# The first block's attention on one core: last queries' scores in the output's bank, and four due times moved

## The chip, the cores and the metric

The kernel runs on one core of one Trainium2 chip. The metric is the device time of one execution in microseconds. TensorE does the matrix products, VectorE (DVE), ScalarE (ACT) and GpSimd (POOL) the rest, SyncE (SP) issues most loads. Each engine works through its own queue in order and waits at semaphores for the others.

## The reference, cut to what matters

Two transformer blocks run one behind the other on 512 tokens of width 1024. The change touches only the attention of the first block: 16 heads of width 64, 16 meta tokens ahead of the 512, a forget gate that adds a difference of running sums to the scores, and an output gate.

```python
def _fox_attend(q_blk, c_q, pos_q, k, v, c_k, pos_k):
    s = jnp.einsum('bhqd,bhkd->bhqk', q_blk, k).astype(jnp.float32) * (FOX_HEAD_DIM ** -0.5)
    s = s + (c_q[..., :, None] - c_k[..., None, :])
    s = jnp.where(pos_k[None, :] <= pos_q[:, None], s, -jnp.inf)
    p = jax.nn.softmax(s, axis=-1)
    return jnp.einsum('bhqk,bhkd->bhqd', p, v.astype(jnp.float32))
```

Queries and keys are normalized per head (mean square, root, gain) before that. Behind it the output is multiplied by `sigmoid(gate)`, goes through `fox_w_out`, and a feed-forward part follows. The second block (gated linear attention and a mixture of 64 experts) isn't touched.

## The kernel before

The method `fox` does the attention. The heads go in eight pairs `t`. For each pair TensorE projects the query (512 columns, one bank), the key and the value (528 columns, two banks each) and the gate (512, one bank), eight pieces of three or six products each; `project` yields after each piece. After each piece a `Weave` advances by one step and runs what is due in that step: `at(delay, fn)` puts a function so many steps ahead. A pair takes 32 steps. The numbers `F_V` to `F_0` in one line of the file, and `K_0` and `Q_1` for the first pairs, are those delays; nothing else sets the order. Each function issues its instructions on all the engines at once, so that its place in the step list is its place in every queue.

- `got_q`, `got_k`: evacuate the projection on VectorE (L392), square on ScalarE (L394) and POOL (L396, L397: a high part and the rest of the square). `root` (due `Q_U` or `K_U` steps later) sums the squares per head on TensorE (`sums`, L323) into a bank `tp`, and starts the root (L222 to L226 on ScalarE, L224 on VectorE). `scaled` (due `Q_R` or `K_R` later) ends the root (L229, L230) and scales the query or key (L406).
- `got_v`: evacuates the value (L416) and transposes it after `F_V` steps (L422, L425, bank `tp`).
- `got_g`: evacuates the gate (L462) and works out its sigmoid in three parts, due `F_G`, `F_G + 2` and `F_G + 6` steps later: L467 and L468 on ScalarE, L472 on ScalarE with L473 and L474 on POOL, L477 on ScalarE.
- `attend(t)`: eight units u = 2i + s (query block i of 128, head s of the pair), one every two steps. `scores` makes the scores in a bank `py` (L502 mask, L504, L506), their maximum on VectorE (L510, L512), the exponential with its sum on ScalarE (L515); `scaled` divides by the sum (L520 to L523, two steps later). The last block's rows are 528 wide, more than a bank, and go in two halves: the second into a bank `tp`. `flip`, eight steps behind `scores`, transposes the probabilities into `tp` (L535) and copies them out (L537 on ScalarE or L539 on VectorE, chosen by `F_E`). `values(i)` multiplies them with the values into the bank `plog` (L547), `F_O` and two steps behind the flips of the block's first head; `gated` multiplies the output by the gate (L553).
- Weights: each chunk's high part is made on ScalarE (L170), its low part on VectorE (L180).

PSUM has eight banks: `mm` three, `py` two, `tp` two, `plog` one. A function that takes a bank waits until what was in it has been read.

Of the kernel before, what the change touches and what calls it, by code (L numbers as in the profile page):

```python
# [20 lines left out]
F32 = mybir.dt.float32  # L21
# [9 lines left out]
P = 128  # L31
D = 1024
KT = D // P
T = 512
# [35 lines left out]

A_W, A_Q, A_K, A_R = 1, 1, 2, 5

F_E = 1, 1, 1, 1, 1, 0, 0, 0


F_V, Q_U, Q_R, Q_H, Q_L, K_U, K_R, K_H, K_L, F_S, F_F, F_O, F_G, F_N, F_0 = 6, 3, 2, 12, 1, 2, 2, 6, 2, 12, 8, 4, 12, 2, 5

K_0, Q_1 = (7, 2, 10, 2), (5, 2, 12, 1)


class Weave:
# [5 lines left out]
    def at(self, delay, fn, *args):  # L87
        self.todo.setdefault(self.step + delay, []).append((fn, args))
# [11 lines left out]
class Net:  # L100
# [147 lines left out]
    def fox(self):  # L248
# [9 lines left out]
        pp = self.pp  # L258

        def mm():  # L260
            return pp.tile([P, T], F32, name="mm", bufs=3)
# [86 lines left out]
        def f_bank():  # L348
            return pp.tile([P, T], F32, name="py", bufs=2)
# [34 lines left out]
        at = w.at  # L384
# [28 lines left out]
        def got_v(t, pv):  # L413
            v1 = wk.tile([P, TM], F32, name="v1", bufs=1)
            for p, o, n in pv:
                nc.vector.tensor_mul(v1[:, o:o + n], p, r1[:, o:o + n])  # L416

            def flip():
                vt = vts[t % 2]
                tp = pp.tile([P, T], F32, name="tp", bufs=2)  # L420
                for j in range(NB):
                    nc.tensor.transpose(tp[:, j * P:(j + 1) * P], v1[:, j * P:(j + 1) * P], self.ident)  # L422
                nc.scalar.activation(vt[:, 0:NB].rearrange("p j d -> p (j d)"), tp, AF.Copy)
                tp = pp.tile([P, T], F32, name="tp", bufs=2)
                nc.tensor.transpose(tp[:NM, :P], v1[:, T:TM], self.ident)  # L425
                nc.vector.tensor_copy(vt[:NM, NB], tp[:NM, :P])

            at(F_V, flip)

        def got_q(t, pq):  # L430

# [54 lines left out]
        def attend(t):  # L486
            vt = vts[t % 2]
            pts, po = [], []

            def scores(i, s):  # L490
                kw = NM + P * (i + 1)
                qi = slice(i * P, (i + 1) * P)
                ps = pp.tile([P, T], F32, name="py", bufs=2)
                if kw > T:
                    n = kw // 2
                    pieces = [(ps, 0, n), (pp.tile([P, T], F32, name="tp", bufs=2), n, n)]
                else:
                    pieces = [(ps, 0, kw)]
                for p, o, n in pieces:
                    m0 = max(o, kw - P)  # L500
                    if m0 < o + n:
                        nc.tensor.matmul(p[:, m0 - o:n], self.identb, self.maskb, start=True, stop=False,  # L502
                                         skip_group_check=True)
                    nc.tensor.matmul(p[:, :n], qs[:, s, qi], kd[:, s, o:o + n], start=(m0 >= o + n), stop=False,  # L504
                                     skip_group_check=True)
                    nc.tensor.matmul(p[:, :n], q2[:, s, qi], k2[:, s, o:o + n], start=False, stop=True,  # L506
                                     skip_group_check=True)
                mx = wk.tile([P, 6], F32, name="mx", bufs=4)
                for e, (p, o, n) in enumerate(pieces):
                    nc.vector.tensor_reduce(mx[:, e:e + 1], p[:, :n], axis=AX.X, op=OP.max, negate=True)  # L510
                if len(pieces) > 1:
                    nc.vector.tensor_tensor(mx[:, 0:1], mx[:, 0:1], mx[:, 1:2], op=OP.min)  # L512
                for e, (p, o, n) in enumerate(pieces):
                    c = pt_off[i] + o
                    nc.scalar.activation(pb[s][:, c:c + n], p[:, :n], AF.Exp, bias=mx[:, 0:1],  # L515
                                         accum_out=mx[:, 2 + e:3 + e])

                def scaled():
                    if len(pieces) > 1:
                        nc.vector.tensor_add(mx[:, 2:3], mx[:, 2:3], mx[:, 3:4])  # L520
                    nc.vector.reciprocal(mx[:, 4:5], mx[:, 2:3])
                    pbi = pb[s][:, pt_off[i]:pt_off[i] + kw]
                    nc.vector.tensor_scalar(pbi, pbi, mx[:, 4:5], None, op0=OP.mult)  # L523

                at(F_N, scaled)

            def flip(i, s):
                if i == 0:
                    pts.append(wk.tile([P, PW], F32, name=f"pt{s}", bufs=1))
                for j0 in range(0, i + 2, 4):  # L530
                    n = min(4, i + 2 - j0) * P
                    c = pt_off[i] + j0 * P
                    tp = pp.tile([P, T], F32, name="tp", bufs=2)
                    for o in range(0, n, P):
                        nc.tensor.transpose(tp[:, o:o + P], pb[s][:, c + o:c + o + P], self.ident)  # L535
                    if F_E[2 * i + s]:
                        nc.scalar.activation(pts[s][:, c:c + n], tp[:, :n], AF.Copy)  # L537
                    else:
                        nc.vector.tensor_copy(pts[s][:, c:c + n], tp[:, :n])  # L539

            def values(i):
                if i == 0:
                    po.append(pp.tile([P, T], F32, name="plog", bufs=1))
                for j in range(i + 2):
                    c = pt_off[i] + j * P
                    for s in range(2):
                        nc.tensor.matmul(po[0][s * HD:(s + 1) * HD, i * P:(i + 1) * P],  # L547
                                         vt[:, j, s * HD:(s + 1) * HD], pts[s][:, c:c + P],
                                         start=(j == 0), stop=(j == i + 1), skip_group_check=True)

            def gated():
                sg = sgs[t]
                nc.vector.tensor_mul(sg, po[0], sg)  # L553
                nc.scalar.activation(ogh[:, t], sg, AF.Copy)

            def gated_lo():
                sg = sgs.pop(t)
                nc.vector.tensor_sub(ogl[:, t], sg, ogh[:, t].bitcast(F32))

            s0 = F_S + (0 if t else F_0)  # L560
            for u in range(2 * NB):
                at(s0 + 2 * u, scores, u // 2, u % 2)
                at(s0 + F_F + 2 * u, flip, u // 2, u % 2)
            for i in range(NB):
                at(s0 + F_F + F_O + 4 * i + 2, values, i)
            at(s0 + F_F + F_O + 4 * NB, gated)
            at(s0 + F_F + F_O + 4 * NB + 2, gated_lo)

        kinds = ((got_q, False), (got_k, True), (got_v, True), (got_g, False))
        forget_1()  # L570
        got_q(0, q0)
# [15 lines left out]
        for n in range(self.EARLY):  # L587
            p = mm() if n < 3 else f_bank()
# [16 lines left out]
        for m in range(KT):  # L605
            if m < self.EARLY:
                p = early[m]
            else:
                p = mm()
# [1041 lines left out]
```

## Time and profile before

| | us |
|---|---|
| median of three runs | 1423.62 |
| lowest, highest | 1423.37, 1426.2 |
| the profiled execution, as timed | 1424.26 |
| its span in the trace | 1422.6 |
| TensorE busy, of the span | 1353.3 (95%) |
| VectorE busy | 742.4 (52%) |
| ScalarE busy | 535.8 (38%) |
| POOL busy | 144.1 (10%) |

The page gives the busy time of each engine and in how much of each fortieth of the span it was busy. TensorE is at nine tenths or more from the third fortieth on; ScalarE and VectorE are at six to eight tenths in the first nine and fall off after that. The first nine fortieths are the attention of the first block. The DMA engines are nearly full only in the last third, the experts.

### The profile page before, as it was taken

To read this page: it belongs to the slowest core of one execution; us is meant where nothing else is said; L and a number is where in the kernel's file an instruction comes from. 1 tells how busy PE (TensorE), PEld (TensorE's weight loads), DVE (VectorE), ACT (ScalarE), POOL (GpSimd) and SP (SyncE) were. 2 spreads that over 40 slices of the span, in tenths; PEclk is the share of its full clock that TensorE was granted. 3 is DMA by queue.
4 is the path that set the end of the run, shared out by engine and by line. 5 is a ranking of instruction groups with operands and counts; after the bars stand their busy time and mean duration, and the time that the engine had idled before them with its cause. 6 is when DMAs were issued, how large, how long until landed. Compare 5 with 4: busy or idle time off the path is not lost.

```text
span 1422.6 us, 20730 instructions
## 1 busy us (share of the span) xinstructions
PE 1353.3 (95%) x8506; PEld 1027.8 (72%) x8506; DVE 742.4 (52%) x1321; ACT 535.8 (38%) x988; POOL 144.1 (10%) x127
## 2 busy tenths in 40 slices
PE   7899999999999999999999999999989999999994
PEld 6788888888788888888887888876556555555542
DVE  7887778774654433444456576542233332333343
ACT  6766666664523212333443444522111111111113
POOL 2212222211200000000322122000000000000001
PEclk9999999999999999999999999999989999999998
DMA  4111111113332322232221223698998999999995
GB/s 168 65 40 60 60 61 60 60 60 119 119 108 89 119 89 89 89 108 99 90 89 63 85 89 118 265 390 351 399 413 347 420 420 421 420 420 421 419 420 213
DMA packets 41346, 282.26 MB, mean 198 GB/s; under 512 B 4736, under 2 KB 4992, under 8 KB 7840
## 3 DMA queue, kind: packets, MB, share of 16 engines
q1 hardware_dynamic: 40464, 280.05, 49.8%
q8 instruction: 68, 1.11, 0.3%
q10 hardware_dynamic: 784, 0.85, 0.2%
q14 instruction: 30, 0.25, 0.0%
HBM read 278.72 MB, written 2.10 MB: 197 GB/s over the span
## 4 chain that ended last, share of the span: by engine, by line
PE 75%; DVE 9%; DMA 8%; ACT 4%; issue 1%; POOL 1%; SPq 0%; ACTq 0%; DVEq 0%; POOLq 0%
PE mm L207 20%; PE mm L336 8%; PE py L207 8%; PE tp L207 8%; PE tp L1269 7%; DMA wring<-in_w_dram 6%; PE mm L1357 6%; PE py L1301 3%; PE mm L792 2%; PE mm L1287 2%; PE mm L1288 2%; PE tp L1280 1%; DMA wraw<-in_w_dram 1%; DVE pb L523 1%; PE plog L547 1%
## 5 line engine op out<-in xcount | busy, mean ns | idle before, releaser
L180 DVE TENSOR_TENSOR whl<-wraw,whl 128x1024 fp32r<-128x1024 f32 x138 | 181.6, 1316 | 102.4 <-ACT whl L170 102.2
L336 PE MATMUL mm<-xh,whl 128*128 128x264 f32 (+1 forms) x736 | 183.4, 333 | 3.8 <-DVE q L392 2.8
L170 ACT ACTIVATE whl<-wraw 128x1024 fp32r<-128x1024 f32 x138 | 144.5, 1050 | 109.6 <-PE mm L207 45.8
L207 PE MATMUL mm<-xh,whl 128*128 128x512 f32 x544 | 175.9, 397 | 0.0
L336 PEld LDWEIGHTS mm<-xh,whl 128*128 128x128 f32 x736 | 120.8, 191 | 19.0 <-issue 3.4
L1269 PEld LDWEIGHTS tp<-h,xt 128*128 128x128 f32 x1024 | 115.9, 192 | 6.1 <-PE mm L1357 2.5
L207 PEld LDWEIGHTS mm<-xh,whl 128*128 128x128 f32 x544 | 102.2, 188 | 23.2 <-issue 2.3
L1269 PE MATMUL tp<-h,xt 128*128 128x128 f32 x1024 | 118.5, 276 | 0.2 <-DVE h L1260 0.2
L207 PE MATMUL mm<-xl,whl 128*128 128x512 f32 x272 | 106.0, 390 | 0.0
L336 PE MATMUL mm<-xl,whl 128*128 128x264 f32 (+1 forms) x368 | 100.1, 325 | 0.0
L1307 DVE SCALAR_TENSOR_TENSOR h<-py,sv,h 128x512 fp32r<-128x512 f32 (+1 forms) x33 | 24.2, 735 | 137.9 <-ACT h L1304 137.9
L1357 PE MATMUL mm<-wring,h 128*32 128x512 f32 x664 | 76.7, 595 | 2.3 <-ACT h L1272 2.0
L1289 DVE TENSOR_TENSOR acc<-acc,mm 128x512 f32<-128x512 f32 (+1 forms) x120 | 73.7, 672 | 7.8 <-PE mm L1288 7.6
L1272 ACT ACTIVATE h<-tp,vecs 128x128 f32<-128x128 f32 x128 | 36.6, 369 | 104.8 <-PE tp L1269 104.8
L1369 ACT ACTIVATE tmp<-mm,sv 128x256 f32<-128x256 f32 x16 | 7.6, 474 | 179.5 <-PE mm L1357 164.4
L207 PE MATMUL mm<-ogh,whl 128*128 128x512 f32 x224 | 73.7, 396 | 0.0
L1287 PE MATMUL mm<-h,ss 128*128 128x512 f32 (+1 forms) x128 | 62.6, 490 | 9.4 <-DVE acc L1289 6.4
L635 POOL TENSOR_TENSOR ss<-ss,sq 128x512 f32<-128x512 f32 x21 | 29.2, 1405 | 371.1 <-ACT sq L631 349.1
L207 PE MATMUL py<-xh,whl 128*128 128x512 f32 x208 | 65.8, 391 | 0.0
L207 PE MATMUL tp<-xh,whl 128*128 128x512 f32 x208 | 65.2, 389 | 0.0
L336 PEld LDWEIGHTS mm<-xl,whl 128*128 128x128 f32 x368 | 62.3, 191 | 3.1
L207 PEld LDWEIGHTS mm<-xl,whl 128*128 128x128 f32 x272 | 51.1, 188 | 11.5 <-issue 1.4
(429 smaller groups left out, 2472.2 us busy)
## 6 DMA issues: line engine op xcount, KB each, us to landing
wring<-in_w_dram SPq DMA_DIRECT2D x124, 1024.0 KB, 19.8
wraw<-in_wd_dram SPq DMA_DIRECT2D x69, 1024.0 KB, 4.8
whl<-in_w_dram SPq DMA_DIRECT2D x27, 1024.0 KB, 16.3
v<-in_w_dram SPq DMA_DIRECT2D x20, 1024.0 KB, 17.6
wraw<-in_w_dram SPq DMA_DIRECT2D x18, 1024.0 KB, 19.8
h<-in_xT_dram SPq DMA_DIRECT2D x8, 256.0 KB, 5.8
acc<-in_w_dram SPq DMA_DIRECT2D x2, 1024.0 KB
out_dram<-wring SPq DMA_DIRECT2D x4, 512.0 KB, 4.5
```

What stands on the lines that cost most here:

```text
L170: self.nc.scalar.activation(hl[:, 0], raw, AF.Copy)
L180: self.nc.vector.tensor_sub(hl[:, 1], raw, hl[:, 0].bitcast(F32))
L207: self.nc.tensor.matmul(out, w, x[:, first + k], start=(at + k == 0 and e == 0), stop=(at + k == of - 1 and e == 2))
L336: nc.tensor.matmul(p[:rows, :m], w[:, wi, k], xx[:, k, o:o + m], start=(n == 0), stop=(n == 3 * KT - 1))
L635: nc.gpsimd.tensor_add(ss, ss, sq)
L792: nc.tensor.matmul(pv[b], x[:, k, bs], w2[:, wi, k % 2], start=(k == 0 and e == 0), stop=(k == KT - 1 and e == 2))
L1269: nc.tensor.matmul(p[:, k], self.xt[:, b, (k0 + k) * P:(k0 + k + 1) * P], oh[:, 1, b], start=(b + k == 0), stop=(b == NB - 1), skip_group_ ...
L1272: nc.scalar.activation(xs[:, k0 + k], p[:, k], AF.Copy, scale=self.vec(V_FN2, k0 + k))
L1287: nc.tensor.matmul(pc, gt[:, b * P:(b + 1) * P], yh[:, hs], start=True, stop=False)
L1289: nc.vector.tensor_add(acc[b][:, hs], acc[b][:, hs] if q else self.xt[:, b, hs], pc)
L1301: nc.tensor.matmul(py[js, o:o + c], hT[:, e, js], w, start=(e == 0), stop=(e == 1), skip_group_check=True)
L1357: nc.tensor.matmul(ps[32 * j:32 * j + 32], xs[:, k, 32 * j:32 * j + 32], self.ring[q, k][:, j * T:(j + 1) * T], start=(k == 0), stop=(k == ...
```

## The change

Six numbers and three places in the code:

- `V_0 = 8`: the first pair's values are transposed eight steps behind their projection, not six.
- `Q_U` 3 to 4, `K_U` 2 to 3: sums of query and key one step later. For the second pair's query `Q_1` goes from (5, 2, 12, 1) to (4, 5, 12, 1): sums one step sooner, scaling three steps later behind them.
- `F_O` 4 to 6: values two steps later, and so the gating.
- `F_G` 12 to 2: all three parts of the gate's sigmoid ten steps sooner.
- `F_E`: the last unit's transposes (u7) are copied out by ScalarE instead of VectorE.
- The second half of the last block's scores goes into `plog`, and of the two exponentials that of the second half comes first.

```diff
-F_E = 1, 1, 1, 1, 1, 0, 0, 0
+F_E = 1, 1, 1, 1, 1, 0, 0, 1
-F_V, Q_U, Q_R, Q_H, Q_L, K_U, K_R, K_H, K_L, F_S, F_F, F_O, F_G, F_N, F_0 = 6, 3, 2, 12, 1, 2, 2, 6, 2, 12, 8, 4, 12, 2, 5
+F_V, Q_U, Q_R, Q_H, Q_L, K_U, K_R, K_H, K_L, F_S, F_F, F_O, F_G, F_N, F_0 = 6, 4, 2, 12, 1, 3, 2, 6, 2, 12, 8, 6, 2, 2, 5
-K_0, Q_1 = (7, 2, 10, 2), (5, 2, 12, 1)
+K_0, Q_1, V_0 = (7, 2, 10, 2), (4, 5, 12, 1), 8
...
-            at(F_V, flip)
+            at(F_V if t else V_0, flip)
...
-                    pieces = [(ps, 0, n), (pp.tile([P, T], F32, name="tp", bufs=2), n, n)]
+                    pieces = [(ps, 0, n), (pp.tile([P, T], F32, name="plog", bufs=1), n, n)]
...
-                for e, (p, o, n) in enumerate(pieces):
+                for e, (p, o, n) in reversed(list(enumerate(pieces))):
```

On TensorE, behind the last query block's scores of the second head in a repeating pair, before the change (`whl` and `xh`, `xl` are the projection's weights and inputs, `pt` the transposed probabilities, `vt` the values, `sqh` and `sql` the squares whose sums are the query's):

```order
L502 MATMUL tp<-maskb,identb 128x128
L504 MATMUL tp<-kd,qs 128x264
L506 MATMUL tp<-k_123,q_122 128x264
L547 MATMUL plog<-pt_982,vt_139 64x128
L547 MATMUL plog<-pt_1002,vt_139 64x128
L547 MATMUL plog<-pt_982,vt_139 64x128
L547 MATMUL plog<-pt_1002,vt_139 64x128
L336 MATMUL mm<-xh,whl 128x264 x2
L336 MATMUL mm<-xl,whl 128x264 x2
L336 MATMUL mm<-xh,whl 128x264 x2
L323 MATMUL tp<-sqh,hones 128x512
```

The same place on TensorE after the change; two projection pieces follow the scores (lines of the code are one higher from here on):

```order
L507 MATMUL plog<-k_123,q_122 128x264
L336 MATMUL mm<-xh,whl 128x264 x2
L336 MATMUL mm<-xl,whl 128x264 x2
L336 MATMUL mm<-xh,whl 128x264 x4
L336 MATMUL mm<-xl,whl 128x264 x2
L336 MATMUL mm<-xh,whl 128x264 x2
L536 MATMUL tp<-ident,pb_128 128x128 x4
L548 MATMUL plog<-pt_985,vt_139 64x128
L548 MATMUL plog<-pt_1008,vt_139 64x128
L548 MATMUL plog<-pt_985,vt_139 64x128
L548 MATMUL plog<-pt_1008,vt_139 64x128
L323 MATMUL tp<-sqh,hones 128x512
```

The first block's value products have moved from right behind the scores to behind the transposes of the next unit (u4), into the bank that the scores have just used, and the query sums stand directly behind them; in a flip's row x4 is one bank.

On VectorE, from the last probability scaling of a pair to the copies of u6 (`q_1169` is the key's evacuation), before the change:

```order
L523 TENSOR_SCALAR pb_129<-pb_129,mx 128x528
L229 TENSOR_TENSOR rs_t<-rs_t,rs_x 128x512
L230 SCALAR_TENSOR_TENSOR rr<-rs_t,rr 128x512
L406 SCALAR_TENSOR_TENSOR q_1022<-q_1022,qg,rr 128x512
L539 COPY pt_1002<-tp 128x512
L392 TENSOR_TENSOR q_1169<-mm,r_119 128x264 x2
L539 COPY pt_982<-tp 128x512
L539 COPY pt_982<-tp 128x128
```

The same place on VectorE after the change, one pair later in the list (`q_1581` is the key's evacuation):

```order
L524 TENSOR_SCALAR pb_129<-pb_129,mx 128x528
L540 COPY pt_1425<-tp 128x512
L229 TENSOR_TENSOR rs_t<-rs_t,rs_x 128x512
L230 SCALAR_TENSOR_TENSOR rr<-rs_t,rr 128x512
L406 SCALAR_TENSOR_TENSOR q_1445<-q_1445,qg,rr 128x512
L392 TENSOR_TENSOR q_1581<-mm,r_119 128x264 x2
L540 COPY pt_1402<-tp 128x512
L540 COPY pt_1402<-tp 128x128
```

The copy of u5 stands ahead of the query's scaling now; the key's evacuation stands behind both in either list.

On POOL, one repeating pair before the change (512 wide is the query, 528 the key, `sg` the gate):

```order
L396 TENSOR_TENSOR sqh<-q_1022 128x512
L397 TENSOR_TENSOR sql<-sq,sqh 128x512
L473 TENSOR_SCALAR sg<-sg 128x512
L474 TENSOR_TENSOR sg<-sg,se 128x512
L396 TENSOR_TENSOR sqh<-q_1169 128x528
L397 TENSOR_TENSOR sql<-sq,sqh 128x528
```

And after it:

```order
L473 TENSOR_SCALAR sg<-sg 128x512
L474 TENSOR_TENSOR sg<-sg,se 128x512
L396 TENSOR_TENSOR sqh<-q_1028 128x512
L397 TENSOR_TENSOR sql<-sq,sqh 128x512
L396 TENSOR_TENSOR sqh<-q_1164 128x528
L397 TENSOR_TENSOR sql<-sq,sqh 128x528
```

The gate's two operations have moved from between query and key to ahead of the query.

## Rows read from the trace of the kernel before

**Rows 1.** Busy us by stretch: PE, PEld, DVE, ACT, POOL; then clock, DMA share, GB/s

```profile
36.00:73.00 37.00, 31.69 (x197) 27.36 (x196) 31.41 (x63) 26.92 (x58) 9.78 (x7) 0.95 0.19 68
...
147.00:184.00 37.00, 36.10 (x271) 31.05 (x269) 29.71 (x62) 24.94 (x52) 8.61 (x7) 1.00 0.17 58
...
371.00:700.00 329.00, 329.00 (x1452) 272.23 (x1451) 152.35 (x181) 98.33 (x122) 10.09 (x9) 1.00 0.28 98
...
63.40:66.80 3.40, 3.35 (x15) 3.35 (x16) 3.33 (x7) 2.89 (x7) 2.39 (x2) 0.50 0.00 0
```

**Rows 2.** Timeline of PE: start us, duration, engine, line, operation; idle before in brackets

```profile
147.84 0.36 PE L323 MATMUL tp<-sqh,hones 128*128 128x264 f32 x1 [0.32 <-DVE pt L539]
148.32 0.39 PE L323 MATMUL tp<-sql,hones 128*128 128x264 f32 x1
...
169.08 0.49 PE L535 MATMUL tp<-ident,pb 128*128 128x128 f32 x3
...
172.29 0.22 PE L502 MATMUL tp<-maskb,identb 128*128 128x128 bf16 x1
...
172.74 0.66 PE L547 MATMUL plog<-pt,vt 128*64 128x128 f32 x8
...
174.16 0.40 PE L323 MATMUL tp<-sqh,hones 128*128 128x512 f32 x1
174.39 0.39 PE L323 MATMUL tp<-sql,hones 128*128 128x512 f32 x1
...
175.90 0.66 PE L535 MATMUL tp<-ident,pb 128*128 128x128 f32 x4 [0.39 <-ACT pb L515]
...
180.77 0.71 PE L535 MATMUL tp<-ident,pb 128*128 128x128 f32 x5
...
183.43 1.09 PE L547 MATMUL plog<-pt,vt 128*64 128x128 f32 x16
```

**Rows 3.** Timeline of DVE in the same stretch

```profile
168.57 0.43 DVE L523 TENSOR_SCALAR pb<-pb,mx 128x400 f32<-128x400 f32 x1
169.28 0.69 DVE L392 TENSOR_TENSOR q<-mm,r 128x512 f32<-128x512 f32 x1 [0.28 <-PE mm L336]
...
171.22 1.48 DVE L523 TENSOR_SCALAR pb<-pb,mx 128x400 f32<-128x400 f32 x1
...
179.38 0.90 DVE L406 SCALAR_TENSOR_TENSOR q<-q,qg,rr 128x512 f32<-128x512 f32 x1
...
180.84 0.77 DVE L392 TENSOR_TENSOR q<-mm,r 128x264 f32<-128x264 f32 x2
```

**Rows 4.** Timeline of ACT in the same stretch

```profile
174.81 0.48 ACT L515 ACTIVATE pb<-py,mx 128x264 f32<-128x264 f32 x1 [1.24 <-DVE mx L520]
175.19 0.19 ACT L515 ACTIVATION_READ_ACCUMULATOR pb<-py,mx 128x1 f32 x1
...
175.64 0.20 ACT L515 ACTIVATION_READ_ACCUMULATOR pb<-tp,mx 128x1 f32 x1
175.74 0.69 ACT L222 ACTIVATE rr<-tp,epsc 128x512 f32<-128x512 f32 x1
```

**Rows 5.** Timeline of POOL in the same stretch

```profile
146.09 2.17 POOL L397 TENSOR_TENSOR sql<-sq,sqh 128x528 fp32r<-128x528 f32 x1
...
171.17 1.30 POOL L397 TENSOR_TENSOR sql<-sq,sqh 128x512 fp32r<-128x512 f32 x1
...
180.70 1.29 POOL L474 TENSOR_TENSOR sg<-sg,se 128x512 f32<-128x512 f32 x1
...
183.09 2.17 POOL L397 TENSOR_TENSOR sql<-sq,sqh 128x528 fp32r<-128x528 f32 x1
```

**Rows 6.** Chain that ended last, in order of time: start us, us, engine, line

```profile
148.95 2.92 PE mm L336 x24
```

**Rows 7.** Timeline of PE in the first pairs: the two long waits

```profile
42.16 0.65 PE L422 MATMUL tp<-ident,v 128*128 128x128 f32 x4 [1.31 <-DVE rs_x L224]
...
63.45 0.59 PE L336 MATMUL mm<-xh,whl 128*128 128x264 f32 x1 [2.84 <-DVE q L392]
```

## The prediction

> **What bounds the kernel now.** I read first the busy time by stretch [rows 1], then the queues of one repeating stretch, engine by engine [rows 2 to 5]. TensorE is busy in all 329 us behind the attention stage, so only a delay or a gain that reaches the end of that stage counts, and it then moves everything behind it by as much: no later TensorE wait is large enough to absorb it, and the late weight loads start when earlier buffers come free. In the attention stage the same 37.0 us repeat from pair to pair; POOL's long subtraction stands at 146.09 and again at 183.09 [rows 5]. TensorE is busy 36.10 of them, which looks full, but its queue shows three waits. Let T be the start of the three transposes at 169.08, right behind a query projection; all times with a T in front count from it.
>
> First wait: the second half of the scores of the last queries, second head (u7), starts at 172.29, about 0.2 late, since one of the two banks tp is held by the first head's exponential. Second: the transposes at 175.90 wait for the same bank ring; the exponential that frees it ends at 175.84 [rows 2, 4]. Third: the key sums at 147.84, idle 0.32 and then another 0.36 (148.32 follows it by 0.48, where such products follow each other by 0.12), because their second product at 148.32 needs POOL's subtraction, which ends at 148.26 [rows 2, 5]. Together some 1.6 us per pair (0.2, 0.4 to 0.5, and 0.7 plus what the pipeline hides). The third wait is the end of a chain that starts at T: query evacuation on VectorE 169.28, maxima of the last scores, exponentials, the query sums' logarithm on ScalarE 175.74, the query scaling on VectorE, the key evacuation 180.84, POOL's two key operations, key sums [rows 3 to 5].
>
> **The change part by part.**
>
> Last queries in the output's bank. The 16 second-half score groups go from tp to plog. No instruction is added. The first two waits lose their cause: the tp ring then holds only transposes and sums. The new wait: plog has one buffer, so the first value products (eight, on plog) must wait for the exponential of u7's second half, which the change puts ahead of that of the first half. That exponential now starts when VectorE has u7's maximum: 174.81, and the piece that is read first would be done with its accumulator row at 175.38 [rows 4]. VectorE is late there for a reason that the change leaves alone: its scaling at 171.22 takes 1.48 beside POOL's subtraction of 171.17, which ends at 172.47 [rows 3, 5]. So plog is free at T + 6.30, and the value products start at about T + 6.35.
>
> The Trainium skill (SBUF — State Buffer, Who interferes with whom) says of this pair of engines that whichever of the two issues first holds a shared pair of ports for its whole instruction and the other is fully blocked. The trace agrees: the 1.48 us row ends 0.23 after POOL's. By that rule POOL's other operations can hold VectorE too, which is a rival below.
>
> Values two steps later, query sums one step later. By the order, TensorE now has the transposes of u4, the value products and the query sums in a row. It comes to the value products earlier than the bank does: 175.90 is T + 6.82; without the value products (0.66), the sums (0.46) and the two waits (0.2 and 0.4 to 0.5), and with the transposes' 0.4, that is about T + 5.4. So it waits some 0.9 to 1.0 us there. That is more than the two waits it replaces (0.2 and 0.4 to 0.5), and the query sums, which today are over at T + 5.70 (174.39 and 0.39), stand behind it: T + 6.35, products 0.66, sums 0.62 (174.16 to 174.78), end T + 7.63 [rows 2]. Today ScalarE takes their logarithm at 175.74, T + 6.66, when the exponentials are through [rows 4]. Now it is T + 7.63: 0.97 later.
>
> From that logarithm to the key evacuation VectorE needs 180.84 - 175.74 = 5.10 us [rows 3, 4], the same instructions before and after; only the copy of u5's transposes goes ahead of the query scaling, and both stand ahead of the key evacuation either way. Today this chain ends just as the key projection does (180.77) [rows 2], so it costs nothing. Now the key evacuation starts at T + 7.63 + 5.10 = T + 12.73 against T + 11.76. From it to the second key sum takes 148.32 + 37.0 - 180.84 = 4.48 today; POOL started 0.25 late there, because the gate's operation (180.70, 1.29) was still on it [rows 5], and that one is moved away, so 4.23. The second key sum comes at T + 16.96 instead of T + 16.24: **0.72 later**.
>
> Key sums one step later. One projection piece (0.73: 24 products take 2.92, a piece is six) [rows 6] now lies ahead of the key sums, and the sixteen value products of the third block (1.09) [rows 2] lie behind them. That shifts 1.09 - 0.73 = **0.36** from before the wait to after it, where no wait covers it: between the key sums at 148.32 and the next T at 169.08 I find no idle row, so those 20.76 us are work. Per pair: 0.72 + 0.36 = 1.08 us. In all six full pairs (T at 95.1, 132.1, 169.1, 206.1, 243.1, 280.1, 37.0 apart): **+6.5 us**.
>
> The gate's sigmoid ten steps sooner. Three ScalarE operations and two POOL operations leave a place where nothing waited for them and go ahead of the query evacuation. ScalarE is busy for 24.94 us of 37 [rows 1] and has room for them; exponentials that it delays by some tenths are used later. On POOL they gain the 0.25 counted above. On VectorE they may block the scaling just ahead of the query evacuation: bounds 0 and the 1.05 us by which the row at 171.22 is longer than its like at 168.57 (0.43); they should be through about when the evacuation starts, so I take 0.15, and give back as much for the query scaling at 179.38, which takes 0.90 beside POOL [rows 3] and would run alone. Net nothing, up to 0.3 either way per pair.
>
> Last copies (u7) from VectorE to ScalarE: two per pair, on an engine with 12 us to spare [rows 1]; the key sums' bank waits for it, but POOL ends later. Nothing.
>
> The first pair. Here the waits are larger: 1.31 at 42.16 and 2.84 at 63.45 [rows 7]. The first goes, since the value transposes move two steps back; but the first scores stand four pieces on and wait for keys that VectorE and ScalarE prepare without TensorE, so it comes back there. The second goes too: the key evacuation no longer stands behind the query scaling. But the order now puts the maxima of u7 behind that query scaling on VectorE, and the transposes of u4, which need the key sums' banks, behind the exponentials of u7. The wait moves some 5 us on. The clock fell to half (1.2 GHz) at the end of the 2.84 us wait for 3.4 us [rows 1], which is 1.7 us of TensorE work; it may do so again. Bounds: -4.2 (both waits gone) and +1.7 (a second fall); I take 0, because the order shows a wait in the place of each.
>
> Sum: 1424.26 (the profiled run: span 1422.6 and 1.7 around it) + 6.5 + 0 = 1430.8. That run is 0.6 above the median of the three, 1423.62; against the median it is 1430.1. I predict 1430.
>
> **The rivals.**
>
> It does what it says (faster). The three waits of 1.6 us vanish and nothing takes their place: 6 x 1.6 = 9.6, 1414. For it: the banks are indeed freed. Against it: the value products would need plog 0.9 us earlier, so u7's maximum as much earlier; that decides, and the row that holds it (171.22) is untouched. Chance 0.10.
>
> The wait moves, but the key evacuation is not late: if VectorE had a little over 1 us more slack between logarithm and key evacuation than the rows show, the second key sum would come when TensorE gets there. The key projection would end at 180.77, T + 11.69, less today's two waits (0.7) and the products that go behind it (0.9), plus the new wait (0.95): T + 11.0. Then come transposes, twelve value products, three projection pieces and transposes again, some 4.3 in all: T + 15.3, and a pair takes 15.3 + 20.76 + 0.36 = 36.4: 6 x 0.6 = 3.6, 1420. Chance 0.18, of it 0.08 faster by more than the bound and 0.10 within.
>
> The start gains: the pairs lose as forecast but the 2.84 us are saved and part of 1.31: 6.5 - 4 = 2.5, 1426. Chance 0.10.
>
> The gate's POOL operations block VectorE in every pair for most of one (1.29): 6 x 1.3 more, 1438. The rows show such blocks (171.22); it decides whether POOL is through when the query projection ends. Chance 0.05.
>
> The Trainium skill (Perfetto Trace Analysis, Optimizing Tensor Performance, Matmuls) asks for independent groups to rotate through banks so that one's evacuation overlaps the next's products. By that rule one bank for both heads' scores and then the output costs a wait wherever an evacuation is late, which is the forecast's first step and speaks for +6.5; a ring of two, as now, costs the 0.2 and 0.4 to 0.5 of the rows. No run here shows the single bank yet.
>
> **How the numbers follow.** Forecast (each pair 0.5 to 1.6 longer, 1427 to 1434): 0.57. Slower by over 0.2% (2.85 us, about what a measurement of this kernel can tell from no change): 0.57 + 0.05 = 0.62. Within: 0.10 + 0.10 = 0.20. Faster: 0.10 + 0.08 = 0.18. The range 1418 to 1435 takes in the forecast, the start rival and the slack rival, and leaves out 1414, 1438 and the edges, together under 0.2. The likeliest case's own range is 1427 to 1434.
>
> **What would show it.** Right: in the repeating stretch TensorE waits for ScalarE's exponential ahead of the value products (about 0.9), the value projection waits for the key evacuation (some 0.7), and the key sums for POOL (about 1); the period is near 38.1; no wait for tp at the transposes of u4. Wrong: a period at or below 37.0. If the first wait is there and the other two are not, the slack rival holds; if the period is as forecast and the sum smaller, the start; if VectorE's scaling ahead of the query evacuation takes over 1 us, the gate rival. If u7's exponential starts well before T + 5.7, the main step is wrong.

## The result

The changed kernel takes 1432.22 us, median of five runs, against 1424.58 for five of the kernel before beside it: 1.0052 times as long, 95% interval 1.0039 to 1.0065, so slower by half a per cent. One of the five was a slow run (1538.73 at a granted clock of 0.857), which the ratio leaves out; the median of the other four is 1431.77. The forecast was 1430, in a range of 1418 to 1435. The profiled execution has a span of 1429.6, 7.0 more than before. T of the eighth pair, the last, came at 317.12 before and comes at 324.07 now, 6.95 later; from there to the end it is 1105.5 in both. In these two executions the whole loss is in the first block's attention, and what comes behind passes it on. The row of T in the eighth pair, before and after:

```profile
317.12 0.49 PE L535 MATMUL tp<-ident,pb 128*128 128x128 f32 x3
...
324.07 0.49 PE L536 MATMUL tp<-ident,pb 128*128 128x128 f32 x3
```

A repeating pair now lasts 38.1 us, against 37.0. By stretch (busy us of PE, PEld, DVE, ACT, POOL; then clock, DMA share, GB/s), one repeating pair of the changed kernel, as in [rows 1]:

```profile
185.00:223.00 38.00, 36.13 (x268) 31.02 (x268) 28.65 (x60) 25.46 (x54) 8.46 (x6) 1.00 0.16 56
```

TensorE is as busy as it was (36.10 of 37.00 before, 36.13 of 38.00 now); the microsecond is idle time. Its waits in the stretch of all full pairs (us in total, times, longest):

```profile
PE plog L548 <- ACT pb L516: 5.9, 6, 1.2
...
PE tp L323 <- POOL sql L397: 3.2, 6, 0.6
...
PE mm L336 <- DVE q L392: 2.4, 6, 0.4
```

Three waits, once in each of the six pairs, and they are the three that the prediction named. The total of the first holds one longer wait of 1.18, in the first of the six pairs. TensorE's timeline of the pair with T = 209.75 (start, duration, operation, idle before):

```profile
209.75 0.49 PE L536 MATMUL tp<-ident,pb 128*128 128x128 f32 x3
...
214.55 0.60 PE L536 MATMUL tp<-ident,pb 128*128 128x128 f32 x4
216.09 0.66 PE L548 MATMUL plog<-pt,vt 128*64 128x128 f32 x8 [0.94 <-ACT pb L516]
...
217.01 0.39 PE L323 MATMUL tp<-sql,hones 128*128 128x512 f32 x1
...
222.84 0.39 PE L336 MATMUL mm<-xh,whl 128*128 128x264 f32 x1 [0.40 <-DVE q L392]
...
226.58 0.39 PE L323 MATMUL tp<-sql,hones 128*128 128x264 f32 x1 [0.56 <-POOL sql L397]
```

The transposes of u4 wait no longer (214.55; in [rows 2] they waited 0.39 at 175.90), but the value products behind them do. What holds them, and the chain that follows, on ScalarE, VectorE and POOL:

```profile
215.47 0.48 ACT L516 ACTIVATE pb<-plog,mx 128x264 f32<-128x264 f32 x1 [0.72 <-DVE mx L521]
215.84 0.19 ACT L516 ACTIVATION_READ_ACCUMULATOR pb<-plog,mx 128x1 f32 x1
...
217.45 0.69 ACT L222 ACTIVATE rr<-tp,epsc 128x512 f32<-128x512 f32 x1 [0.46 <-PE tp L323]
...
211.88 1.48 DVE L524 TENSOR_SCALAR pb<-pb,mx 128x400 f32<-128x400 f32 x1
...
221.69 0.75 DVE L406 SCALAR_TENSOR_TENSOR q<-q,qg,rr 128x512 f32<-128x512 f32 x1
222.36 0.77 DVE L392 TENSOR_TENSOR q<-mm,r 128x264 f32<-128x264 f32 x2
...
211.84 1.30 POOL L397 TENSOR_TENSOR sql<-sq,sqh 128x512 fp32r<-128x512 f32 x1
...
224.35 2.17 POOL L397 TENSOR_TENSOR sql<-sq,sqh 128x528 fp32r<-128x528 f32 x1
```

Read from the top: u7's exponential at 215.47 lets the value products go, the query sums end at 217.40, their logarithm starts 0.05 later, the key evacuation at 222.36 stands right behind the query's scaling, and POOL's subtraction (224.35 + 2.17) ends 0.06 before the second key sum.

### The profile page after: what moved, and what is told of

It is laid out like the page before. It is cut to its first block, busy times and chain, and to the rows that moved or that the text cites. A ratio compares the mean times of both kernels' runs of the same rounds, so it can differ in the third digit from the quotient of the medians.

```text
span 1429.6 us, 20724 instructions
## 1 busy us (share of the span) xinstructions
PE 1353.7 (95%) x8506; PEld 1028.6 (72%) x8506; DVE 735.7 (51%) x1305; ACT 539.7 (38%) x1004; POOL 143.1 (10%) x127
## 4 chain that ended last, share of the span: by engine, by line
PE 72%; DMA 11%; DVE 9%; ACT 4%; issue 1%; POOL 1%; ACTq 0%; SPq 0%; DVEq 0%; POOLq 0%
PE mm L207 20%; PE py L207 8%; PE tp L207 8%; DMA wring<-in_w_dram 7%; PE mm L336 7%; PE tp L1270 6%; PE mm L1358 5%; PE py L1302 3%; PE mm L793 2%; PE plog L548 2%; PE mm L1288 1%; DVE pb L524 1%; DMA v<-in_w_dram 1%; DMA wraw<-in_w_dram 1%; PE mm L1289 1%
```

## The experiments

The theory to be tested has two statements. The one bank makes the value products wait and so makes the query sums late. And a pair lasts as long as the chain from T to the second key sum, plus the TensorE work behind it, so that what is late in the chain is late in the pair. The main rivals: the loss is in the gate's operations or in the sums' later places. Twelve kernels were run; where no number of runs is given, the time is that of a single run. "A pair" is the distance of one T from the next in the trace, and the argument goes by it: from the last T to the end, where none of these kernels differs, the traces have from 1103.3 to 1107.2 us, and the first T lies between 56.9 and 60.9, so single wholes that are a few microseconds apart decide little.

**The bank undone.** The changed kernel with the second half back in tp:

```diff
-                    pieces = [(ps, 0, n), (pp.tile([P, T], F32, name="plog", bufs=1), n, n)]
+                    pieces = [(ps, 0, n), (pp.tile([P, T], F32, name="tp", bufs=2), n, n)]
```

> The changed kernel with one part undone: the second half of the last scores goes to tp again; all the delays and the order of the exponentials stay. Theory (the value products wait for the bank, the query sums stand behind them, and the key chain is late by as much): the value products do not wait any more, but the query sums now take the bank that u7's exponential frees at T + 6.1 to 6.3, so they end at about T + 6.95 in place of T + 7.65; the second key sum comes about 0.7 earlier, and a pair takes 37.4 us (37.2 to 37.6) against 38.1. In six pairs 4 us less than the changed kernel, about 1428. Rival (the bank does not matter; the loss is the gate's operations on POOL or the key sums' later place): 38.1 us again, 1432.

Measured: 1428.12, a pair 37.58 to 37.60, the upper end of what was expected. The value products do not wait; the query sums (T = 209.06) end at 216.20, T + 7.14. The two waits behind them stay, 0.4 and 0.5:

```profile
215.81 0.39 PE L323 MATMUL tp<-sql,hones 128*128 128x512 f32 x1
...
PE tp L323 <- POOL sql L397: 2.7, 5, 0.5
PE mm L336 <- DVE q L392: 1.9, 5, 0.4
```

So the bank is worth 0.5 of the 1.1 us, and it acts through the query sums. The rest is not the bank's: the second key sum stands at T + 16.30 here, only 0.06 behind the kernel before, and the tail behind it is 21.27 in place of 20.76.

**The bank and the values alone, in the kernel before.** Values two steps later, second half in plog, its exponential first:

```diff
-... 2, 12, 8, 4, 12, 2, 5
+... 2, 12, 8, 6, 12, 2, 5
-(pp.tile([P, T], F32, name="tp", bufs=2), n, n)]
+(pp.tile([P, T], F32, name="plog", bufs=1), n, n)]
-                for e, (p, o, n) in enumerate(pieces):
+                for e, (p, o, n) in reversed(list(enumerate(pieces))):
```

> The kernel before with one part of the change alone: second half of the last scores in plog, its exponential first, values and gating two steps later; sums, gate, copies and first pair as before. Theory (a pair lasts as long as the chain from T to the second key sum, plus the work behind it): the query sums are not behind the values, so the logarithm stays at T + 6.6 and the second key sum at T + 16.2; but the sixteen value products of the third block (1.09 us) now stand behind the key sums, so the tail is 20.76 + 1.09 = 21.85 and a pair takes 38.05 us (37.8 to 38.2), as long as with the whole change, with no wait at the value projection. Rival (the loss is the later sums): 37.0 or less, since the two waits for tp are gone.

Measured: 1431.64, a pair 38.2, as slow as the whole change, with the query sums early. In the pair with T = 210.92, TensorE and POOL:

```profile
226.89 0.36 PE L323 MATMUL tp<-sqh,hones 128*128 128x264 f32 x1 [0.77 <-DVE pt L539]
227.12 0.39 PE L323 MATMUL tp<-sql,hones 128*128 128x264 f32 x1
...
229.13 1.09 PE L547 MATMUL plog<-pt,vt 128*64 128x128 f32 x16
...
224.90 2.17 POOL L397 TENSOR_TENSOR sql<-sq,sqh 128x528 fp32r<-128x528 f32 x1
```

The second key sum stands at T + 16.20 (16.2 expected) and POOL's subtraction ends 0.05 before it; the sixteen products of the third block (1.09) stand behind it now. That fits the account of chain plus tail with another chain and another tail; the tail is 22.00, 0.15 longer than the 21.85 expected. The value products wait here too, 0.46 for u7's exponential, but the query sums stand ahead of them. One thing was not expected: two waits are put down to VectorE's copies of the transposes (0.86 and 0.77). They cover the same time as the chain, so this run alone does not tell which of the two holds the key sums.

**u7's maximum ahead of u5's scaling.** The changed kernel with one line moved on VectorE:

```diff
-                at(F_N, scaled)
+                at(F_N + 2 if (i, s) == (NB - 2, 1) else F_N, scaled)
```

> The changed kernel with one thing moved: VectorE scales u5's probabilities (the 1.48 us row beside POOL) two steps later, behind the maximum of u7. Theory: u7's exponential starts about 1.0 earlier (T + 4.7 in place of T + 5.72), the wait of the value products falls from 0.94 shown to under 0.2, the query sums end at T + 6.6 to 6.7, the waits at the value projection (0.40) and at the key sums (0.54) stay as they are, since chain and TensorE move together; a pair takes 37.1 us (36.9 to 37.3), the whole about 1426. Rival (the value products are late for another reason, or the loop does not go through the query sums): 38.1 or only some tenths less.

Measured: 1424.41, a pair 37.27. The wait of the value products is gone, the two others are what they were:

```profile
PE tp L323 <- POOL sql L397: 2.7, 5, 0.6
PE mm L336 <- DVE q L392: 2.0, 5, 0.4
...
212.89 0.66 PE L548 MATMUL plog<-pt,vt 128*64 128x128 f32 x8
...
211.83 0.43 DVE L524 TENSOR_SCALAR pb<-pb,mx 128x400 f32<-128x400 f32 x1
```

The value products go at T + 5.52 (212.89, T = 207.37), 0.82 sooner, and the pair is 0.83 shorter. So the bank costs what it does only since u7's maximum is late. The whole is 1.6 below the 1426 expected; of the 6.9 that the profiled runs lie apart, 2.0 are behind the last T, where the two kernels are the same. The moved row takes 0.43 here, no longer beside POOL's subtraction, against 1.48.

**The key's evacuation ahead of the query's scaling.** The changed kernel, from the third pair on:

```diff
-(Q_U, Q_R, Q_H, Q_L)
+(Q_U, Q_R if t == 0 else Q_R + 2, Q_H, Q_L)
```

> The changed kernel with one thing moved: from the third pair on (queries 2 to 7) the query's scaling comes two steps later, so that on VectorE the key's evacuation stands ahead of it. Theory (the key chain is late since it stands behind the query's): the wait of the value products stays (0.94), but the key evacuation starts with the end of the key projection, about T + 11, 1.6 us earlier, and the waits at the value projection (0.40 shown) and at the key sums (0.54 shown) vanish; a pair takes 36.65 us (36.4 to 36.9), below the 37.0 of the kernel before; in six pairs 9 less than the changed kernel, about 1423. Rival (the loss is in the bank alone): 38.1, 1432.

Measured: 1422.00, a pair 36.63, within 0.02 of the forecast. Only the first wait is left, and the evacuation (T = 206.34) starts at T + 10.94:

```profile
PE plog L548 <- ACT pb L516: 4.7, 5, 0.9
...
217.28 0.77 DVE L392 TENSOR_TENSOR q<-mm,r 128x264 f32<-128x264 f32 x2 [0.42 <-PE mm L336]
```

So both later waits (0.40 and 0.56 as listed) came from the key's chain standing behind the query's, and a pair is 1.47 shorter without them. With that one order changed the pair is shorter than the 37.0 of the kernel before.

**Both moves together.**

> The changed kernel with both moves on VectorE together: u5's scaling behind u7's maximum, and from the third pair on the query's scaling behind the key's evacuation. Theory (two separate waits: the one bank at the value products, and the key chain behind the query's): the gains add up, no TensorE wait of over 0.2 is left in a pair, and a pair takes 36.63 (with the second move alone) less the 0.94 shown and some 0.1 to 0.3 that the pipeline hides, 35.4 to 35.7 us; the whole 1422.0 - 6 x 1.1 = about 1415 (1414 to 1417). Rival (the chain of the key binds again as soon as the first wait is gone): 36.3 to 36.6, 1420 to 1422.

Measured: a pair 35.80, no TensorE wait listed from the third pair on, 1417.02 in four runs: 0.9953 of the kernel before (0.9937 to 0.997). The gains add: 38.1 - 35.8 = 2.3, where the single moves gave 0.83 and 1.47. The pair is 0.1 above the expected band.

**The gate's sigmoid back at twelve steps**, in the changed kernel and, below, in the one with both moves (`F_G` 2 to 12 in the line of numbers):

> The changed kernel with the gate's sigmoid where it was (12 steps). Theory (the gate's place costs and gives nothing much): the value products wait 0.94 as before, a pair takes 38.1 us (38.0 to 38.35, the upper end if POOL's gate operation holds the key's first operation by up to 0.25), the whole 1431 to 1433. Rival (its operations on POOL, ahead of the query, block VectorE and make u7's exponential late): 37.0 to 37.6, 1425 to 1429.

Measured: 1447.96, a pair 39.8 to 40.5. Neither theory held; the gate's old place is much worse in the new order. In the pair with T = 217.92, VectorE, POOL and TensorE:

```profile
228.95 1.79 DVE L229 TENSOR_TENSOR rs_t<-rs_t,rs_x 128x512 f32<-128x512 f32 x1
...
228.92 1.28 POOL L474 TENSOR_TENSOR sg<-sg,se 128x512 f32<-128x512 f32 x1 [1.66 <-ACT se L472]
...
232.73 0.39 PE L336 MATMUL mm<-xh,whl 128*128 128x264 f32 x1 [2.10 <-DVE q L392]
```

The query's logarithm comes at 226.25, T + 8.33 in place of T + 7.70, as ScalarE has the gate's operations ahead of it; then POOL's gate operation issues 0.03 ahead of a step of the query's root, which takes 1.79 in place of 0.68. The key's evacuation is 1.71 later, the wait at the value projection 2.10 in place of 0.40. The Trainium skill (SBUF — State Buffer, Who interferes with whom) says that a VectorE instruction with two inputs in SBUF contends with a GpSimd instruction that reads SBUF, and that the order of issue decides which of the two blocks; the rows agree, since POOL issued first and the blocked step ends 0.54 after POOL's.

Not all of the 2.3 us is the chain's. One of the six pairs takes 39.82, 1.71 more than in the changed kernel and as much as the evacuation is late; over it the granted clock is 1.00. The other five take 40.4 to 40.5, with the clock at 0.96 over the pair: behind their wait of 2.10 it falls to its lower level for a while, which is 0.6. A stretch that starts in the pair of 39.82, and one of the others (the third figure from the end is the clock):

```profile
147.00:185.00 38.00, 34.44 (x254) 29.29 (x253) 29.23 (x59) 23.93 (x52) 6.84 (x5) 1.00 0.15 56
185.00:223.00 38.00, 35.91 (x257) 31.49 (x256) 28.32 (x55) 23.81 (x49) 8.33 (x6) 0.96 0.16 57
```

> The changed kernel with both moves on VectorE, and the gate's sigmoid back where it was (12 steps). Theory (the gate's old place cost 2.3 a pair since its ScalarE operations go ahead of the query's root and its POOL operation blocks VectorE at the query's scaling, both ahead of the key's evacuation): with the query's scaling behind the key's evacuation they are off the path, and a pair takes 35.8 to 36.2 us, 1417 to 1419.5. Rival (the gate's old place costs by itself, on POOL, which the key's operations must share): 37 to 38, 1424 to 1431.

Measured: 1419.11, a pair 35.62 to 35.64, somewhat shorter than the 35.80 with the gate early. So the gate's place costs nothing by itself; it costs where it falls into the key's chain. The sum is no smaller: T of the second pair comes 38.6 behind that of the first, against 34.7, since POOL now holds the first pair's key sums 1.32 us and the clock is at 0.50 to 0.69 from 68 to 80 us.

**The query's scaling later in the kernel before.** As above, `Q_R + 2`:

> The kernel before with the second move alone (from the third pair on the query's scaling two steps later). Theory (there the key's evacuation starts as the projection ends, 180.77 against 180.84, so that the query's scaling ahead of it costs nothing): 37.0 us for a pair (36.8 to 37.1), the whole 1423.5 to 1425. Rival (the query's scaling ahead of the key's evacuation costs in either kernel): 36.4 or less, about 1420.

Measured: 1427.36, a pair 38.23. This run did not do what was meant: the sums stand one step sooner in that kernel, so the scaling two steps later is still ahead of the key's evacuation, and now beside the gate. VectorE and POOL, T = 207.69:

```profile
219.45 1.57 DVE L406 SCALAR_TENSOR_TENSOR q<-q,qg,rr 128x512 f32<-128x512 f32 x1
220.94 0.76 DVE L392 TENSOR_TENSOR q<-mm,r 128x264 f32<-128x264 f32 x2
...
219.03 1.45 POOL L474 TENSOR_TENSOR sg<-sg,se 128x512 f32<-128x512 f32 x1
```

The evacuation is at T + 13.25 in place of T + 11.76, 1.49 later, and a pair is 1.23 longer. The 0.26 between them is not slack. POOL's gate operation ends at 220.48, ahead of the evacuation, and so no longer holds up the key's operations on POOL as in [rows 5]. From the evacuation to the second key sum takes 4.22 in place of 4.48, and that sum stands at T + 17.47 against T + 16.24, 1.23 later:

```profile
225.16 0.39 PE L323 MATMUL tp<-sql,hones 128*128 128x264 f32 x1
...
222.93 2.17 POOL L397 TENSOR_TENSOR sql<-sq,sqh 128x528 fp32r<-128x528 f32 x1
```

So in the kernel before the key chain has no slack, as the prediction had it; the slack rival needed over 1.

**Both moves in the kernel before** (`Q_R + 3` there):

> The kernel before with both moves on VectorE, as the changed kernel had them: u5's scaling behind u7's maximum, and from the third pair on the query's scaling behind the key's evacuation (three steps later here, since its sums come one step sooner). Theory (the two moves and the change each take away a wait of their own): u7's exponential is 0.8 to 1.0 earlier, so the 0.39 wait at the transposes of u4 goes, and the key chain starts with the end of the projection; the 0.2 for the second half of u7 and POOL's gate operation ahead of the key stay, so a pair takes 36.2 to 36.6 us and the whole 1419 to 1422, more than the changed kernel with the same moves (35.8, 1417). Rival (the change is worth nothing beside the two moves): 35.8 as well, 1416 to 1418.

Measured: 1441.3 in four runs, a pair 40.5: a miss in the other direction. TensorE and VectorE, T = 215.30:

```profile
233.38 0.36 PE L323 MATMUL tp<-sqh,hones 128*128 128x264 f32 x1 [3.26 <-DVE pt L539]
...
230.75 0.75 DVE L406 SCALAR_TENSOR_TENSOR q<-q,qg,rr 128x512 f32<-128x512 f32 x1
231.42 1.22 DVE L180 TENSOR_TENSOR whl<-wraw,whl 128x1024 fp32r<-128x1024 f32 x1
232.55 0.88 DVE L539 COPY pt<-tp 128x512 f32<-128x512 f32 x2
```

The key sums need the bank that the copy of u7 frees. In the kernel before that copy is VectorE's, and the moved scaling and a weight's low part now stand ahead of it. In the change ScalarE makes it. With that one number of `F_E` changed too:

> The kernel before with both moves on VectorE and one more part of the change: ScalarE copies out u7's transposes. Theory (in the run without it the key sums waited 3.26 us for the bank that VectorE's copy of u7, 232.55, frees behind the query's scaling and a weight's low part): that wait goes to at most 0.7, since POOL ends its second key operation about then; of the waits of the kernel before the 0.2 at u7's second half stays, and a pair takes 36.0 to 36.6 us, the whole 1418 to 1422. If it is as short as the changed kernel with both moves (35.6 to 35.8, 1415 to 1417), the bank of the change is worth nothing beside the three moves of VectorE's work. Rival (the key sums are late for another reason than that copy): 38 or more, 1432.

Measured: 1415.97 in five runs, 0.9955 of the kernel before (0.9941 to 0.9969), a pair 35.65 to 35.9, no wait listed in the repeating pairs. So the last case named there holds: beside these three moves the rest of the change (the bank, the later values and sums, the gate, the first pairs) is together worth nothing that can be measured (35.80 and 1417.02 with it).

**The first pairs.** The changed kernel with both moves, and `Q_1` with 7, then with 8 (and the use one step later):

```diff
-K_0, Q_1, V_0 = (7, 2, 10, 2), (4, 5, 12, 1), 8
+K_0, Q_1, V_0 = (7, 2, 10, 2), (4, 7, 12, 1), 8
```

> As the run before, and in the first pairs the second pair's query is scaled two steps later (7 in place of 5), so that VectorE takes the maximum of u7 ahead of it. Theory (the 4.08 us wait at 69.65 is the query's scaling of 2.1 us ahead of u7's maximum, so that the exponentials and behind them the root of the keys and the bank are late): the wait falls by about 2, to 1.6 to 2.1, and the clock, which falls at its end now, may stay up; T of the second pair comes 2 to 3 earlier than in the run before, and the whole is 1412 to 1413.5. Rival (the bank is late for another reason): no difference to the run before.

> The changed kernel with both moves, and the second pair's query scaled three steps later than in the change (8, its use one step later too), so that on VectorE the copy that frees the keys' bank goes ahead of the query's scaling as well. Theory (of the 2.51 us wait that is left at 69.17, the scaling's 2.1 us hold the bank from 67.13, when the root has read it, to 68.69): the wait falls to about 1.0, and T of the second pair comes 1.5 earlier; the whole 1412 to 1413.5, a little under the 1414.7 of the version with 7. Rival (the clock's fall behind the wait, and not the wait, sets the start): no difference, 1414 to 1415.

Measured: 1414.68 (four runs; 0.9935 of the kernel before, 0.9919 to 0.9952) and 1415.34 (five runs; 0.9929, 0.9914 to 0.9944). The long wait in the changed kernel, with both moves, with 7, and with 8:

```profile
69.65 0.68 PE L536 MATMUL tp<-ident,pb 128*128 128x128 f32 x4 [4.08 <-DVE rs_x L224]
```

```profile
67.54 0.86 PE L536 MATMUL tp<-ident,pb 128*128 128x128 f32 x4 [3.61 <-DVE rs_x L224]
```

```profile
69.17 1.12 PE L536 MATMUL tp<-ident,pb 128*128 128x128 f32 x4 [2.51 <-DVE rs_x L224]
```

```profile
66.95 0.66 PE L536 MATMUL tp<-ident,pb 128*128 128x128 f32 x4 [0.61 <-DVE rs_x L224]
```

With 7 the wait falls by less than expected (2.51 left, not 1.6 to 2.1), with 8 by more (0.61 left, not 1.0; another of 0.95 for a copy of VectorE's stands at 73.15 then). The whole does not follow: the two medians are 0.7 apart in the wrong direction, and both versions' runs lie between 1413.7 and 1418.5. In the profiled runs the second T comes 34.65 behind the first with 7, as without it (34.68), and 31.60 with 8. The profiled run with 7 was the slowest of its four (1418.46, the others 1414.2 to 1415.0), with the clock at its lower level from 68 to 74 us, where the run without the edit has it from 68 to 71; what the start of the others looks like no trace shows. That stays open. These are the lowest medians of all, 0.65 and 0.71% below the kernel before; between them the runs do not decide.

| kernel | a pair, us | whole, us |
|---|---|---|
| before | 37.0 | 1424.58 |
| changed | 38.1 | 1432.22 |
| changed, bank undone | 37.6 | 1428.12 |
| before, bank and values alone | 38.2 | 1431.64 |
| changed, u5's scaling later | 37.3 | 1424.41 |
| changed, query's scaling behind the key | 36.6 | 1422.00 |
| changed, both moves | 35.8 | 1417.02 |
| changed, gate back | 40.4 | 1447.96 |
| changed, both moves, gate back | 35.6 | 1419.11 |
| before, query's scaling later | 38.2 | 1427.36 |
| before, both moves | 40.5 | 1441.3 |
| before, both moves, u7's copy on ScalarE | 35.7 | 1415.97 |
| changed, both moves, first pair 7, 8 | 35.8 | 1414.68, 1415.34 |

## Why the prediction was right, point by point

**The wait at the value products.** Forecast: exponential of u7 about T + 5.73, bank free at T + 6.30, products at T + 6.35, a wait of 0.9 to 1.0. In the trace: T + 5.72, T + 6.28, T + 6.34, and 0.94. The two later waits, forecast at some 0.7 and about 1, are listed with 0.40 and 0.56; the starts on either side of them are 0.78 and 0.92 apart (222.06 to 222.84, 225.66 to 226.58). The run with u5's scaling moved shows the cause.

**The chain.** Query sums over at T + 7.63; T + 7.65. Key evacuation at T + 12.73; T + 12.61, as VectorE needs 4.91 from the logarithm in place of 5.10: the query's scaling takes 0.75, not the 0.90 of [rows 3], now that the gate's operation is not beside it (the prediction gave this 0.15 back, but set it against a loss). From there to the second key sum 4.23; 4.22. The sum at T + 16.96; T + 16.83.

**The tail.** 20.76 + 0.36 = 21.12; 38.10 - 16.83 = 21.27. The two errors, -0.13 and +0.15, cancel, which is luck: 38.08 forecast, 38.1 measured. The 0.15 is a mis-sized term. The sixteen value products were counted as 1.09, the length of their row, but cost more between the projection's products. In the pair with T = 171.64:

```profile
189.44 0.40 PE L336 MATMUL mm<-xh,whl 128*128 128x264 f32 x2
189.77 1.09 PE L548 MATMUL plog<-pt,vt 128*64 128x128 f32 x16
...
191.14 0.41 PE L336 MATMUL mm<-xl,whl 128*128 128x264 f32 x2
```

From 189.44 to 191.14 are 1.70 us. Four projection products lie in them, 0.49 at 0.73 for a piece of six, which leaves 1.21 for the sixteen, 0.12 more than counted; the run with the bank and the values alone has the same 0.15 too much in its tail. That the account itself holds, and did not only come out so, is shown by the runs that moved one end of it: 36.65 forecast for the query's scaling and 36.63 measured, 37.1 and 37.27 for u5's.

**The gate.** The step "net nothing, up to 0.3 either way" was mis-sized as the worth of this edit. Among the other edits the gate's old place costs 40.4 - 38.1 = 2.3 a pair, 1.7 of it the chain and 0.6 the clock; what it is worth in the kernel before no run shows. The forecast of the whole change did not suffer, since it took the chain from rows that the gate hardly touched; the kernel with all but this edit was forecast at 1431 to 1433 by the same account and took 1447.96. The 0.15 that the step set for VectorE ahead of the query evacuation is 0 in five of the six pairs, where the evacuation starts at T + 0.20 as before, and 0.49 in the first of them (see below).

**The last copies on ScalarE.** "Nothing" fits the changed kernel, where ScalarE's copy ends at 225.69 and POOL at 226.52, but no run undid that number alone there. The two runs of the kernel before with both moves show what it is worth in another order: 40.5 against 35.7, of which 1.5 is the clock (last section). That POOL ends later than the copy, the reason given, is true only while the copy stands ahead of the query's scaling.

**The first pair.** Forecast: net nothing, a wait in the place of each. T of the second pair comes at 94.95, against 95.06 in the kernel before. The 1.31 came back as 1.17 at the first scores, the 2.84 as 4.08 at the transposes of u4; a third wait of the kernel before that the prediction did not count, 1.08 at its first key sums (69.64), is gone. The clock ran at its lower level (1.2 GHz) behind that wait: between 70 and 72 us it was 0.54.

**What was missing.** The second pair, the first of the six, took 38.59, half a microsecond more than the others, which the sum had as equal: 0.5 of the 6.95. It is the gate rival in one pair of six. POOL, then VectorE, around T = 94.95:

```profile
94.21 1.28 POOL L474 TENSOR_TENSOR sg<-sg,se 128x512 f32<-128x512 f32 x1 [0.60 <-ACT se L472]
...
94.43 1.29 DVE L524 TENSOR_SCALAR pb<-pb,mx 128x400 f32<-128x400 f32 x1
95.64 0.68 DVE L392 TENSOR_TENSOR q<-mm,r 128x512 f32<-128x512 f32 x1
```

The gate's operation is still on POOL there; the scaling beside it takes 1.29 where its like in [rows 3] takes 0.43, and the query evacuation starts at T + 0.69, 0.49 late. The second key sum is late by as much (T + 17.31). With the gate back, in the kernel with both moves, that pair is as short as the others (35.64); in every run with the gate early it is about 0.48 longer. The profiled run came out at 1431.3 where the sum was 1430.8.

**The rivals.** That it does what it says fell with the first wait, and the slack rival with the two later waits and with the run that moved the key's chain late in the kernel before. The start gained nothing. The gate blocks VectorE in the other pairs too, at 209.24 (0.76 beside POOL), but it is over when the query evacuation can start.

## What to carry to other kernels

In a loop whose busiest engine looks full, look for the chain that goes once around through all engines, and count a pair as that chain plus the work behind its end: taking waits from the busy engine gives nothing while the chain is as long, and work moved behind the chain's end costs its full time in the queue, which here was a little more than the length of its row. Look in the queues of the other engines for work that stands ahead of a step of the chain and is not needed soon; two such moves on VectorE took 2.3 us from a pair of the changed kernel, and the same two cost 3.5 in the kernel before until one copy went to ScalarE as well. The worth of an edit is that in its order: the gate's old place cost 2.3 us a pair in the changed kernel and saved 0.2 beside the two moves.

## What the hardware showed that was not expected

The clock's lower level has a price in this loop that can be read off. In the kernel before with both moves, the key sums wait 3.25 us in every pair, but two of the six, the first and the fifth, took 38.96 and 38.97 and the others 40.49 to 40.51. Three stretches, each right behind such a wait (the last three figures: clock, DMA share, GB/s):

```profile
233.00:238.00 5.00, 4.62 (x26) 4.65 (x27) 2.95 (x7) 3.98 (x8) 0.00 (x0) 0.68 0.64 213
274.00:279.00 5.00, 5.00 (x50) 4.68 (x51) 2.99 (x5) 4.46 (x8) 0.00 (x0) 1.00 0.62 213
313.00:318.00 5.00, 5.00 (x30) 4.86 (x30) 3.02 (x6) 4.50 (x8) 0.00 (x0) 0.66 0.62 213
```

Behind 273.89 the clock stayed up, and that pair, the fifth, was 1.5 us shorter, with 50 products in five microseconds in place of 26 and 30. So of the 3.5 that this kernel loses to 37.0 a pair, 1.5 are the clock behind the wait, and the same wait does not always bring it down; why it did not there, no run shows. Behind the waits of 2.10 us with the gate back it fell in five of six pairs. Behind waits of 0.9 to 1.2 us (the changed kernel, and the one before with the query's scaling later) no stretch of the pairs from 147 to 299 us shows a fall.
